# The last token tiles of a mixer: T1's work first, sums beside copies, and a fixed place for the last transposes

## The chip, the cores and the metric

One core of a Trainium2 chip runs the whole program. The metric is the device time of one execution in microseconds (us), lower is better. The engines are PE (TensorE), DVE (VectorE), ACT (ScalarE), POOL (GpSimd) and SP (SyncE, which only issues DMAs here). Each takes its own instructions in the order in which the program lists them.

## The reference

One layer of a decoder trunk on x, 1024 tokens by 1024 channels, in float32: a pooling mixer, then a gated feed-forward network (FFN) with hidden width 2816.

```
h = rms_norm(x, norm_mix_g)
d = per group of 256 channels: causal window mean of h (windows 2, 4, 8, 16) - h
x = x + scale * (einsum(d, pool_w) + pool_b)                 # the mixer
u = causal_depthwise_conv(rms_norm(x, norm_ffn_g) @ w_in)    # 3 taps, 1024 -> 2 x 2816
val, gate = split(u)
x = x + (silu(gate) * val) @ w_out                           # 2816 -> 1024
```

## The kernel before

**The mixer** runs over 8 tiles of 128 tokens (`j` = 0 to 7). For each tile `mixer_window` makes window means on PE (bank `psd`), `mixer_out` the group product (bank `psy`) and DVE adds it to x (L265), which gives the tile `x` that the FFN starts from; it is also stored to DRAM. `rstd_of` takes its mean square (ACT, `junk_b`) and a few operations on one column (`st_b`, L159 to L163), and `ffn_norm` scales the tile (L276, L277) into `n2_j`. `ffn_operand` turns `n2_j` on PE (eight transposes into two banks, `pst_j`, L292) and brings it into `n2f`, where channels lie on partitions.

**The FFN's products** are done by a seven-product scheme of 2 x 2 blocks, with sums of input blocks in place of the eighth product. Of the tokens' side the operands are B11, B21, B22 and the sums T1 to T4 (T1 = B11 - B12, in `n2f`); tiles 0 to 3 are one half of the tokens, 4 to 7 the other, so T1 is whole only when tile 7 has been turned. Of the weights' side they are A11, A12, A22 and the sums S1 to S4 of each block `n` of 128 hidden columns (`win`). Each product is in float32 accuracy by two halves: `split` and `split_n` make a high half on ACT (L76, L311) and a low half, the difference, on DVE (L77, L312), and `product` runs 12 matmuls of 128x512 (three for each of four slices). `STEPS` names a product's operands and its bank:

```
"P1": ("A11", "B11", "X"), "P6": ("S2", "T2", "Y"), "P5": ("S1", "T1", "Z"), "P2": ("A12", "B21", "X"),
"P7": ("S3", "T3", "Y"), "P3": ("S4", "B22", "Z"), "P4": ("A22", "T4", "Y"),
```

P6, P7 and P4 add up in one bank Y, P5 and P3 in one bank Z, P1 and P2 in X. Between two of them DVE or ACT reads what is there: after P1 ACT copies `q1` (L395); after P5 DVE makes `r` (L406); after P6 `q2` (L401, `q` in the profile); after P7 and P4 the halves of `hb` (L409, L414). PE may not go on adding to the bank before that read. `gated` then does the convolution and the gate: for `val` and for `gate` an ACT pass (L419) and two DVE passes (`conv`, L420 and L421), Silu on ACT, a DVE product, and the store.

**The order.** The program is not written engine by engine: a scheduling layer puts each engine's instructions in order, by their dependences and the order of the code; `tc.issue_after(m)` asks that what is in its block be issued after instruction `m`. `events` lists the products: P1 and P2 of blocks 0 and 1 first, which run while the mixer still works on its last tiles, then P5 and P3 of both, P6, P7 and P4 of each, and from block 2 on all seven block by block. `prep_event(k + LOOK)` prepares the operand of a later product at each step.

The third part of the kernel, the product with `w_out` (L723), is scheduled by its own list and is not touched.

Of the kernel before, what the change touches and what calls it, by code (L numbers as in the profile page):

```python
# [18 lines left out]
NS = S // P  # L19
# [29 lines left out]
def trunk_kernel(ctx: ExitStack, tc: tile.TileContext, x, consts, par, rows, pool_w, w_in, w_out, out):  # L49
# [223 lines left out]
    def ffn_norm(j):  # L273
        x1, r = n2s[j]
        n2 = n2s[j] = pp.tile([P, D], F32, tag="n2", name=f"n2_{j}", bufs=2)
        nc.vector.tensor_tensor(r[1], r[0], r[1], ALU.mult)  # L276
        nc.vector.scalar_tensor_tensor(n2, x1, r[1], gains[0], op0=ALU.mult, op1=ALU.mult)  # L277

# [8 lines left out]

    def ffn_operand(j):
        n2 = n2s.pop(j)
        ps = bank2(f"pst{j}")  # L290
        for c in range(NK):
            nc.tensor.transpose(ps[:, c * P : (c + 1) * P], n2[:, c * P : (c + 1) * P], ident)  # L292
# [9 lines left out]
        b11, b12, b21, b22 = n2f[:, lo, cols0], ps3[:, lo, :], n2f[:, hi, cols0], n2f[:, hi, cols]  # L302
        nc.scalar.activation(b22, ps3[:, hi, :], AF.Copy)
        sub(b11, b11, b12)
        split_n(nops["T1"], b11, cols0)
        sub(n2f[:, lo, cols], b22, b12)
        sub(b21, b22, b21)

    def split_n(t, src, cols=slice(None), ks=slice(None)):
        h = t[:, 0, ks, cols]  # L310
        nc.scalar.activation(h, src, AF.Copy)  # L311
        nc.vector.tensor_tensor(t[:, 1, ks, cols], src, h.bitcast(F32), ALU.subtract)  # L312

# [8 lines left out]
    def sub(out, a, b):  # L322
        nc.vector.tensor_tensor(out, a, b, ALU.subtract)  # L323

    def add(out, a, b):
        nc.vector.tensor_tensor(out, a, b, ALU.add)  # L326

# [20 lines left out]
    def prep_in(n, op):  # L348
        a11, a12, a21, a22 = (raws[n][:, i, k * NH : (k + 1) * NH] for i in range(2) for k in range(2))
        if op in ("S1", "S2") and (n, "S3") not in sums:  # L350
            s3 = sums[n, "S3"] = tmp(f"S3_{n}")
            add(s3, a11, a21)
            add(a21, a21, a22)
        if op in ("S2", "S4") and (n, "S2") not in sums:
            sums[n, "S2"] = a11
            add(a11, a21, a11)
        if op == "S4" and (n, "S4") not in sums:
            add(a12, a12, a11)
        if op == "S3":
            src = sums[n, "S3"]  # L360
        else:
            src = {"A11": a11, "A12": a12, "S1": a21, "A22": a22, "S2": a11, "S4": a12}[op]
        aops[n, op] = split(src, f"{op}s_{n}")
        if op == "A22" and n + 2 < NF:
            load_in(n + 2)

    def product(bank, a, b, opens):
        m = 0
        for k in range(4):
            ks = slice(k * P, (k + 1) * P)  # L370
            for i, l in ((0, 0), (0, 1), (1, 0)):
                nc.tensor.matmul(bank, a[:, i, ks], b[:, l, k, :], start=opens and m == 0, stop=m == 11, skip_group_check=not opens)  # L372
                m += 1

# [8 lines left out]

    def step(n, p):
        a, b, z = STEPS[p]
# [4 lines left out]
        bank = banks[n, z]  # L390
        product(bank, aops.pop((n, a)), nops[b], opens)
        tt = nc.vector.tensor_tensor
# [50 lines left out]

    def event(k):
        if k >= 4:
            prep_event(k + LOOK)
        n, p = events[k]
        step(n, p)
        if p == "P4":
            gated(n)  # L450
# [38 lines left out]
    for j in range(2, NS + 4):  # L489
# [4 lines left out]
        if 1 <= j - 2 < NS:  # L494
            mixer_out(j - 2)
        if 0 <= j - 2 < NS:
            with tc.issue_after(marks["dh1+"]):
                ffn_norm(j - 2)
        if 0 <= j - 4 < NS:
            ffn_operand(j - 4)  # L500
        if j in (4, 6):
# [5 lines left out]
        if j in (7, 8):  # L507
            sums_in(j - 7, 1)
        if j in (8, 10, 11):
            event((8, 10, 11).index(j))  # L510
        with tc.issue_after(marks["edges"]):
# [16 lines left out]
    event(4)  # L528
    for ks in halves:
        split_n(nops["B22"], b22[:, ks], ks=ks)  # L530
    event(5)
# [276 lines left out]
```

## Time and profile before

| | us |
|---|---|
| timed runs, median | 703.62 |
| timed runs, lowest and highest | 703.33, 790.45 |
| profiled execution, own time | 702.61 |
| its span, first to last instruction | 700.9 |

In the profile PE is busy for 99% of the span, DVE for 86%, ACT for 49%. A matmul's record is longer than the time that it adds to PE's stream, since matmuls overlap, so busy time there says little; starts are the better measure. Names in a row are the program's, without numbers: `q` is any `q1` or `q2`, `n` any `n2_j`, `T` any of T1 to T4, `B` any of B11, B21, B22. A row's brackets give the idle time of its engine ahead of it, and the instruction that ended that.

The stretch that the change touches lies from about 58 us (the transposes of tile 4) to about 130 us (block 2's products); of 700.9 us the rest is the mixer's first tiles, the other blocks, and the product with `w_out`.

### The profile page before, as it was taken

Reading aid. Unit: us, or ns where it says so; the run is one execution under the profiler, and the core shown is the slowest. Engines: PE = TensorE matmul, PEld = TensorE weight load, DVE = VectorE, ACT = ScalarE, POOL = GpSimd, SP = SyncE. Lnnn points to the kernel's source line nnn. Section 1 sums busy time; section 2 is a strip of 40 time slices with the busy share of each in tenths; the row PEclk is TensorE's granted clock in tenths of the full one; section 3 lists DMA queues with packets and bytes.
Section 4 is the critical chain, followed back from the end, with each engine's and each line's share of the span. In section 5 each row is a group of like instructions: output and inputs, shape, how many; then the busy total and the mean of one; then the engine's idle time right before and its main releaser. Section 6 shows DMA issues by size and latency. Waiting matters only on the chain.

```text
span 700.9 us, 8493 instructions
## 1 busy us (share of the span) xinstructions
PE 693.9 (99%) x3154; PEld 573.7 (82%) x3154; DVE 600.5 (86%) x885; ACT 343.2 (49%) x515; POOL 12.5 (2%) x30
## 2 busy tenths in 40 slices
PE   8999999999999999999999999999999999999998
PEld 5898778888888888888888888888888888888886
DVE  5688999999888888888988888876887988999985
ACT  4786545454444444444545454454554444444431
POOL 3110000000000000000000000000000000000000
PEclk9999999999999999999999999999999999999999
DMA  9854112232222112222222212229989700122131
GB/s 307 302 141 121 57 65 91 89 122 91 67 84 74 60 78 90 91 90 91 91 90 91 86 65 91 91 84 338 335 305 335 277 22 1 61 90 87 64 106 60
DMA packets 32555, 85.47 MB, mean 122 GB/s; under 512 B 3689, under 2 KB 5377, under 8 KB 29698
## 3 DMA queue, kind: packets, MB, share of 16 engines
q1 hardware_dynamic: 31296, 82.82, 32.8%
q0 software_dynamic: 1184, 2.11, 1.8%
q8 instruction: 24, 0.39, 0.2%
q14 instruction: 17, 0.14, 0.1%
q10 hardware_dynamic: 34, 0.01, 0.0%
HBM read 62.89 MB, written 19.92 MB: 118 GB/s over the span
## 4 chain that ended last, share of the span: by engine, by line
PE 96%; DVE 2%; DMA 1%; ACT 1%; issue 0%; ACTq 0%; DVEq 0%
PE oP L723 30%; PE Y L372 26%; PE Z L372 17%; PE X L372 16%; PE psy L259 3%; PE psd L180 2%; DMA bias_hl<-rows_raw 1%; PE pst L292 1%; PE psy L262 1%; DVE n2f L323 0%; DMA x<-in_x_dram 0%; DVE T L312 0%; PE ps_edges L180 0%; PE ps_gain L227 0%; DVE n L277 0%; DVE S4s L77 0%
## 5 line engine op out<-in xcount | busy, mean ns | idle before, releaser
L723 PE MATMUL oP<-oBP,oAP 128*128 128x512 f32 (+1 forms) x924 | 208.8, 388 | 0.0
L723 PEld LDWEIGHTS oP<-oBP,oAP 128*128 128x128 f32 x924 | 172.9, 188 | 36.0 <-DVE oBP L77 0.3
L372 PE MATMUL Z<-T,S1s 128*128 128x512 f32 x264 | 64.0, 390 | 1.4 <-ACT T L311 1.2
L372 PE MATMUL X<-B,A11s 128*128 128x512 f32 x264 | 64.3, 390 | 0.0
L372 PE MATMUL Y<-T,S2s 128*128 128x512 f32 x264 | 64.0, 390 | 0.0
L372 PE MATMUL X<-B,A12s 128*128 128x512 f32 x264 | 63.5, 389 | 0.0
L372 PE MATMUL Y<-T,S3s 128*128 128x512 f32 x264 | 63.4, 389 | 0.0
L372 PE MATMUL Y<-T,A22s 128*128 128x512 f32 x264 | 63.4, 389 | 0.0
L372 PE MATMUL Z<-B,S4s 128*128 128x512 f32 x264 | 63.2, 389 | 0.0
L372 PEld LDWEIGHTS Z<-T,S1s 128*128 128x128 f32 x264 | 49.3, 188 | 12.6 <-ACT T L311 1.6
L372 PEld LDWEIGHTS Y<-T,S2s 128*128 128x128 f32 x264 | 49.4, 188 | 10.8 <-ACT S2s L76 0.4
L372 PEld LDWEIGHTS Y<-T,S3s 128*128 128x128 f32 x264 | 49.5, 188 | 10.3
L372 PEld LDWEIGHTS Z<-B,S4s 128*128 128x128 f32 x264 | 49.5, 188 | 10.3
L372 PEld LDWEIGHTS Y<-T,A22s 128*128 128x128 f32 x264 | 49.5, 188 | 10.3
L372 PEld LDWEIGHTS X<-B,A12s 128*128 128x128 f32 x264 | 49.5, 188 | 10.2
L372 PEld LDWEIGHTS X<-B,A11s 128*128 128x128 f32 x264 | 49.4, 188 | 10.2
L76 ACT ACTIVATE oBP<-blk 128x512 fp32r<-128x512 f32 x53 | 33.5, 633 | 49.1 <-PE oP L723 32.2
L77 DVE TENSOR_TENSOR oBP<-blk,oBP 128x512 fp32r<-128x512 f32 x53 | 36.6, 691 | 13.3 <-ACT oBP L76 13.3
L430 ACT ACTIVATE gate<-gate 128x1024 f32<-128x1024 f32 x22 | 23.3, 1061 | 44.5 <-DVE gate L421 44.5
L76 ACT ACTIVATE oAP<-blk 128x512 fp32r<-128x512 f32 x55 | 34.1, 621 | 19.2 <-DVE blk L323 15.9
L326 DVE TENSOR_TENSOR win<-win 128x512 f32<-128x512 f32 x60 | 41.3, 688 | 1.1
L77 DVE TENSOR_TENSOR oAP<-blk,oAP 128x512 fp32r<-128x512 f32 x55 | 37.7, 685 | 2.6 <-ACT oAP L76 2.6
(128 smaller groups left out, 941.4 us busy)
## 6 DMA issues: line engine op xcount, KB each, us to landing
win<-in_w_in_dram SPq DMA_DIRECT2D x22, 1024.0 KB, 4.8
g_dram<-val SPq DMA_DIRECT2D x22, 512.0 KB, 2.7
blk<-g_dram SPq DMA_DIRECT2D x33, 256.0 KB, 5.4
blk<-in_w_out_dram SPq DMA_DIRECT2D x31, 256.0 KB, 5.6
A12s<-g_dram SPq DMA_DIRECT2D x22, 256.0 KB, 5.3
B21s<-in_w_out_dram SPq DMA_DIRECT2D x22, 256.0 KB, 2.6
x<-in_x_dram SPq DMA_DIRECT2D x8, 512.0 KB, 7.0
x_dram<-x SPq DMA_DIRECT2D x8, 512.0 KB, 2.6
```

Of the source, the lines that this page charges most:

```text
L76: nc.scalar.activation(t[:, 0, :], src, AF.Copy)
L77: m = nc.vector.tensor_tensor(t[:, 1, :], src, t[:, 0, :].bitcast(F32), ALU.subtract)
L180: m = nc.tensor.matmul(ps[:, c * P : (c + 1) * P], src[:, c * P : (c + 1) * P], weights[:, c // 2, :], start=True, stop=True)
L259: nc.tensor.matmul(o, dh[:, c, :], wps[:, c, :], start=c % 4 == 0, stop=False, skip_group_check=True)
L262: m = nc.tensor.matmul(ps[:, cols], ones, bias_hl[:, cols], start=False, stop=True, skip_group_check=True)
L292: nc.tensor.transpose(ps[:, c * P : (c + 1) * P], n2[:, c * P : (c + 1) * P], ident)
L326: nc.vector.tensor_tensor(out, a, b, ALU.add)
L372: nc.tensor.matmul(bank, a[:, i, ks], b[:, l, k, :], start=opens and m == 0, stop=m == 11, skip_group_check=not opens)
L430: nc.scalar.activation(gate, gate, AF.Silu)
L723: nc.tensor.matmul(bank, a[:, u, i * P : (i + 1) * P], b[:, v, c], start=opens and first, stop=g == NP2 - 1 and m == 2, skip_group_check=n ...
```

## The change

Eight things change, all in the code around the mixer's last tiles.

- `ffn_operand` is cut in two: `ffn_turn` (the transposes, and for tiles 4 to 7 the copy of the upper four slices on ACT) and `ffn_operand` (the rest). `ffn_last` holds the last sum, on B21.
- In `ffn_operand` the two sums that read the transposes' bank come first, then T1's split; for tiles 6 and 7 `ffn_last` is left for later.
- The norm of tile 7 is issued after T1's split of tile 5; the transposes of tile 6 and 7 get a place by hand: tile 7's stand inside block 0's P2, behind three of its four slices (`between`).
- The operands of P5 (S1 of blocks 0 and 1) are prepared right after tile 6's norm.
- `gated(0)` is issued after block 2's S2 sum.
- B22 is split right after T1's last split, ahead of the sums on B21 and of the other preparations; before, it stood behind `event(4)`.
- The pool `ps_yz` gives out one bank, named "lower", that nothing uses, before Z's first banks.
- `event(3)` is issued after the last transposes.

```diff
+    def ffn_turn(j):
         n2 = n2s.pop(j)
         ps = bank2(f"pst{j}")
         for c in range(NK):
-            nc.tensor.transpose(ps[:, c * P : (c + 1) * P], n2[:, c * P : (c + 1) * P], ident)
-        cols = slice(j * P, (j + 1) * P)
-        ps3 = ps.rearrange("p (c s) -> p c s", c=NK)
+            m = nc.tensor.transpose(ps[:, c * P : (c + 1) * P], n2[:, c * P : (c + 1) * P], ident)
+        marks["turned"] = m.ins
+        turned[j] = ps.rearrange("p (c s) -> p c s", c=NK)
+        if j >= NS // 2:
+            nc.scalar.activation(n2f[:, 4:, j * P : (j + 1) * P], turned[j][:, 4:, :], AF.Copy)
+        return m.ins
+
+    def ffn_operand(j, last=True):
+        ps3, cols = turned[j], slice(j * P, (j + 1) * P)
...
-        nc.scalar.activation(b22, ps3[:, hi, :], AF.Copy)
         sub(b11, b11, b12)
-        split_n(nops["T1"], b11, cols0)
-        sub(n2f[:, lo, cols], b22, b12)
-        sub(b21, b22, b21)
+        m = sub(n2f[:, lo, cols], b22, b12)
+        if last:
+            m = ffn_last(j)
+        with tc.issue_after(m):
+            marks[f"T1_{j}"] = split_n(nops["T1"], b11, cols0)
...
+    def ffn_last(j):
+        b21, b22 = (n2f[:, 4:, t * P : (t + 1) * P] for t in (j - NS // 2, j))
+        return sub(b21, b22, b21)
...
-    def product(bank, a, b, opens):
-        m = 0
+    def product(bank, a, b, opens, between):
+        m, order = 0, nullcontext()
         for k in range(4):
             ks = slice(k * P, (k + 1) * P)
-            for i, l in ((0, 0), (0, 1), (1, 0)):
-                nc.tensor.matmul(bank, a[:, i, ks], b[:, l, k, :], start=opens and m == 0, stop=m == 11, skip_group_check=not opens)
-                m += 1
+            with order:
+                for i, l in ((0, 0), (0, 1), (1, 0)):
+                    last = nc.tensor.matmul(bank, a[:, i, ks], b[:, l, k, :], start=opens and m == 0, stop=m == 11, skip_group_check=not opens)
+                    m += 1
+            if between and k == 2:
+                with tc.issue_after(last.ins):
+                    order = tc.issue_after(between())
...
-        if p == "P4":
+        if p == "P4" and n == 0:
+            with tc.issue_after(marks["S2_2"]):
+                gated(n)
+        elif p == "P4":
             gated(n)
...
+        if j == 9:
+            ffn_turn(5)
+            with tc.issue_after(marks[7]):
+                ffn_operand(5)
+            with tc.issue_after(marks["T1_5"]):
+                ffn_norm(7)
+        elif j == 10:
+            ffn_turn(6)
+        else:
...
+        if j == 8:
+            with tc.issue_after(marks["n2_6"]):
+                prep_event(4)
+                prep_event(5)
+            event(0)
+        if j == 10:
+            event(1)
+        if j == 11:
+            event(2, between=lambda: ffn_turn(7))
+            with tc.issue_after(marks["n2_7"]):
+                ffn_operand(6, last=False)
+                with tc.issue_after(marks["T1_6"]):
+                    ffn_operand(7, last=False)
...
+    ps_yz.tile([P, NH], F32, tag="Y", name="lower")
...
-    for k in range(4, 4 + LOOK):
-        with tc.issue_after(marks[NS - 1]):
-            prep_event(k)
...
-    event(3)
+    with tc.issue_after(marks["T1_7"]), tc.issue_after(marks["split_hi"]):
+        prep_event(6)
+        for ks in halves:
+            m = split_n(nops["B22"], b22[:, ks], ks=ks)
+    with tc.issue_after(m):
+        for j in (6, 7):
+            ffn_last(j)
+        for k in range(7, 4 + LOOK):
+            prep_event(k)
+    with tc.issue_after(marks["turned"]):
+        event(3)
     event(4)
-    for ks in halves:
-        split_n(nops["B22"], b22[:, ks], ks=ks)
     event(5)
```

How the engines' orders move is shown at three places; in these rows names carry their numbers (a number behind a name's last `_` is the buffer's).

PE before, from tile 6's transposes to the first products into Z (`X0` is block 0's bank X, and so on):

```order
L292 MATMUL pst6_713<-cst_81,n2_6_637 128x128 x8
L372 MATMUL X1_728<-B11_162,A11s_1_546 128x512 x12
L372 MATMUL X0_660<-B21_164,A12s_0_600 128x512 x12
L372 MATMUL X1_728<-B21_164,A12s_1_655 128x512 x3
L292 MATMUL pst7_743<-cst_81,n2_7_695 128x128 x8
L372 MATMUL X1_728<-B21_164,A12s_1_655 128x512 x9
L372 MATMUL Z0_819<-T1_163,S1s_0_787 128x512
L372 MATMUL Z1_843<-T1_163,S1s_1_790 128x512
L372 MATMUL Z0_819<-T1_163,S1s_0_787 128x512 x11
```

PE after the change, the same place:

```order
L294 MATMUL pst6_719<-cst_81,n2_6_637 128x128 x8
L388 MATMUL X1_729<-B11_162,A11s_1_546 128x512 x12
L388 MATMUL X0_666<-B21_164,A12s_0_600 128x512 x9
L294 MATMUL pst7_753<-cst_81,n2_7_716 128x128 x8
L388 MATMUL X0_666<-B21_164,A12s_0_600 128x512 x3
L388 MATMUL X1_729<-B21_164,A12s_1_655 128x512 x12
L388 MATMUL Z0_824<-T1_163,S1s_0_660 128x512 x12
L388 MATMUL Z1_844<-T1_163,S1s_1_663 128x512 x12
```

Tile 7's transposes move ahead by six matmuls, and the two products into Z no longer mix.

DVE before, behind the sum of tile 7 (`x7`), which stands right ahead of these rows:

```order
L77 TENSOR_TENSOR S1s_0_787<-win0_415,S1s_0_787 128x512
L323 TENSOR_TENSOR n2f_161<-n2f_161,pst5_698 128x4x128 x2
L323 TENSOR_TENSOR n2f_161<-n2f_161 128x4x128
L160 TENSOR_SCALAR st_b7_689<-st_b7_689 128x1
L312 TENSOR_TENSOR T1_163<-n2f_161,T1_163 128x4x128
L162 SCALAR_TENSOR_TENSOR st_b7_689<-st_b7_689 128x1
L323 TENSOR_TENSOR n2f_161<-n2f_161,pst6_713 128x4x128
L163 RECIPROCAL st_b7_689<-st_b7_689 128x1
L323 TENSOR_TENSOR n2f_161<-n2f_161,pst6_713 128x4x128
L276 TENSOR_TENSOR st_b7_689<-st_b7_689 128x1
L323 TENSOR_TENSOR n2f_161<-n2f_161 128x4x128
L277 SCALAR_TENSOR_TENSOR n2_7_695<-x7_152,st_b7_689,gain_b_266 128x1024
```

DVE after the change, from the place where S1's two low halves now stand:

```order
L77 TENSOR_TENSOR S1s_0_660<-win0_415,S1s_0_660 128x512
L77 TENSOR_TENSOR S1s_1_663<-win1_540,S1s_1_663 128x512
L265 TENSOR_TENSOR x7_152<-psy7_681,x7_152 128x1024
L337 TENSOR_TENSOR n2f_161<-n2f_161,pst5_701 128x4x128 x2
L337 TENSOR_TENSOR n2f_161<-n2f_161 128x4x128
L160 TENSOR_SCALAR st_b7_695<-st_b7_695 128x1
L326 TENSOR_TENSOR T1_163<-n2f_161,T1_163 128x4x128
L162 SCALAR_TENSOR_TENSOR st_b7_695<-st_b7_695 128x1
L163 RECIPROCAL st_b7_695<-st_b7_695 128x1
L276 TENSOR_TENSOR st_b7_695<-st_b7_695 128x1
L277 SCALAR_TENSOR_TENSOR n2_7_716<-x7_152,st_b7_695,gain_b_266 128x1024
```

Both S1 halves move ahead of `x7`, and the sums of tile 6 move from between the one-column steps to behind `n2_7`.

DVE before, around the read of Y2 after block 2's P6 (`q2_2`), in the midst of blocks 1 and 2 (`hb1` and `gate33` are block 1's, `r_2` block 2's):

```order
L414 TENSOR_TENSOR hb1_1011<-q1_1_741,Y1_980 128x512
L77 TENSOR_TENSOR S4s_2_1041<-win2_841,S4s_2_1041 128x512
L77 TENSOR_TENSOR A22s_2_1059<-win2_841,A22s_2_1059 128x512
L401 TENSOR_TENSOR q2_2_1077<-Y2_1064,q1_2_1057 128x512
L420 SCALAR_TENSOR_TENSOR gate33_1033<-hb1_1011,par_sb_121,gate33_1033 128x1023
L77 TENSOR_TENSOR A11s_3_1079<-win3_897,A11s_3_1079 128x512
L421 SCALAR_TENSOR_TENSOR gate33_1033<-hb1_1011,par_sb_121,gate33_1033 128x1022
L406 TENSOR_TENSOR r_2_1095<-q1_2_1057,Z2_1082 128x512
```

DVE after the change, the same place:

```order
L433 TENSOR_TENSOR hb1_1012<-q1_1_742,Y1_981 128x512
L440 SCALAR_TENSOR_TENSOR val11_1030<-ha1_819,par_sb_121,val11_1030 128x1022
L340 TENSOR_TENSOR win2_842<-win2_842 128x512
L439 SCALAR_TENSOR_TENSOR gate33_1034<-hb1_1012,par_sb_121,gate33_1034 128x1023
L77 TENSOR_TENSOR S4s_2_1042<-win2_842,S4s_2_1042 128x512
L440 SCALAR_TENSOR_TENSOR gate33_1034<-hb1_1012,par_sb_121,gate33_1034 128x1022
L77 TENSOR_TENSOR A22s_2_1060<-win2_842,A22s_2_1060 128x512
L420 TENSOR_TENSOR q2_2_1078<-Y2_1065,q1_2_1058 128x512
```

The two passes on `gate33` move from behind `q2_2` to ahead of it.

More of the change, by code (lines that the diff above doesn't have):

```diff
@@ L286, in trunk_kernel @@
         nops[b] = nop_tile(nop_a, b)
-    def ffn_operand(j):
+    turned = {}
+    def ffn_turn(j):
         n2 = n2s.pop(j)
@@ L322, in sub @@
     def sub(out, a, b):
-        nc.vector.tensor_tensor(out, a, b, ALU.subtract)
+        return nc.vector.tensor_tensor(out, a, b, ALU.subtract).ins
     def add(out, a, b):
-        nc.vector.tensor_tensor(out, a, b, ALU.add)
+        return nc.vector.tensor_tensor(out, a, b, ALU.add).ins
     def tmp(name):
@@ L355, in prep_in @@
             sums[n, "S2"] = a11
-            add(a11, a21, a11)
+            marks[f"S2_{n}"] = add(a11, a21, a11)
         if op == "S4" and (n, "S4") not in sums:
@@ L382, in small, with step @@
         return work.tile([P, NH], F32, tag=tag, name=name, bufs=bufs)
-    def step(n, p):
+    def step(n, p, between=None):
         a, b, z = STEPS[p]
@@ L390, in step @@
         bank = banks[n, z]
-        product(bank, aops.pop((n, a)), nops[b], opens)
+        product(bank, aops.pop((n, a)), nops[b], opens, between)
         tt = nc.vector.tensor_tensor
@@ L442, in prep_event, with event @@
             prep_in(n, STEPS[p][0])
-    def event(k):
+    def event(k, between=None):
         if k >= 4:
@@ L447, in event @@
         n, p = events[k]
-        step(n, p)
-        if p == "P4":
+        step(n, p, between)
+        if p == "P4" and n == 0:
+            with tc.issue_after(marks["S2_2"]):
+                gated(n)
+        elif p == "P4":
             gated(n)
@@ L495, in trunk_kernel @@
             mixer_out(j - 2)
[L496 to L500, printed above, removed]
+        if j == 9:
[7 more added lines that the diff above has]
+        else:
+            if 0 <= j - 2 < NS:
+                with tc.issue_after(marks["dh1+"]):
+                    ffn_norm(j - 2)
+            if 0 <= j - 4 < NS - 1:
+                ffn_turn(j - 4)
+                ffn_operand(j - 4)
         if j in (4, 6):
```

10 lines of the change are left out of this document (4 added, 6 removed).

## The prediction

> **What bounds the kernel now.** I read the page first, then the chain of work that ended last.
>
> ```profile
> PE 693.9 (99%) x3154; PEld 573.7 (82%) x3154; DVE 600.5 (86%) x885; ACT 343.2 (49%) x515; POOL 12.5 (2%) x30
> PE 96%; DVE 2%; DMA 1%; ACT 1%; issue 0%; ACTq 0%; DVEq 0%
> ```
>
> TensorE (PE) is the path for 96% of the span, so whatever moves the end must lengthen or shorten a stretch in which PE waits or restarts. The chain leaves PE for some 12 us near 67 to 79.5 us: work of VectorE (DVE) and ScalarE (ACT) that ends in T1's last low half.
>
> ```profile
> 72.77 1.28 DVE n L277
> 78.80 0.67 DVE T L312
> 79.51 10.71 PE Z L372 x46
> ...
> 118.30 2.73 PE Y L372 x12
> ```
>
> PE is not idle all that time. Its timeline there (start, length, idle time and what ended it in brackets), and the one row of PE on which the sum below ends:
>
> ```profile
> 75.01 2.33 PE L372 MATMUL X<-B,A12s 128*128 128x512 f32 x9
> 78.55 0.73 PE L372 MATMUL Z<-T,S1s 128*128 128x512 f32 x2 [1.21 <-ACT T L311]
> 79.51 5.27 PE L372 MATMUL Z<-T,S1s 128*128 128x512 f32 x22 [0.23 <-DVE T L312]
> ...
> 118.14 2.89 PE L372 MATMUL Y<-T,S3s 128*128 128x512 f32 x12
> ```
>
> One matmul adds 2.73 / 12 = 0.227 us to the chain. From 75.01 to 79.51 PE started nine matmuls and two more, and 11 x 0.227 = 2.50 of those 4.50 us: **2.0 us is all that there is to win here**, 1.44 us of it shown as idle. Besides these two, the list of what PE waited for has three entries, all at the kernel's start:
>
> ```profile
> PE idle_ps L130 <- DVE eps_t L108: 1.3, 1, 1.3
> PE psy L259 <- ACT dh L244: 0.6, 1, 0.6
> ...
> PE psy L262 <- DMA bias_hl<-rows_raw: 0.2, 1, 0.2
> ```
>
> Before asking whether the change wins the 2.0 us, I ask which engine is behind it: from x7's sum at 66.37 us on, DVE waits for nothing but 0.1 us at a `q`.
>
> ```profile
> DVE x L265 <- PE psy L262: 1.4, 1, 1.4
> L401 DVE TENSOR_TENSOR q<-Y,q 128x512 f32<-128x512 f32 x3 | 2.0, 683 | 0.1
> ```
>
> So DVE, not PE, is short of time from 66 to 118 us. PE follows it wherever a bank must be read before PE may add to it again. The place that matters is `q2_2`: DVE must read Y2 after P6 before PE may start P7 into Y2.
>
> ```profile
> 117.24 0.68 DVE L401 TENSOR_TENSOR q<-Y,q 128x512 f32<-128x512 f32 x1
> 117.84 1.27 DVE L420 SCALAR_TENSOR_TENSOR gate<-hb,par_sb,gate 128x1023 f32<-128x1023 f32 x1
> 119.03 0.68 DVE L77 TENSOR_TENSOR A11s<-win,A11s 128x512 fp32r<-128x512 f32 x1
> ```
>
> `q2_2` ends at 117.92, and P7 starts at 118.14: now 0.2 us are to spare. The first of two `gate` operations stands right behind it, the second behind A11s.
>
> **The change, part by part.** I take DVE's queue from x7's sum to `q2_2`, since DVE takes its instructions in order and had no slack there.
>
> *What stands in it.* By the order, 67 instructions lie between the two before and 67 after. Two go, S1s_0 and S1s_1: the change puts both ahead of x7's sum, into the wait in brackets.
>
> ```profile
> 66.37 1.22 DVE L265 TENSOR_TENSOR x<-psy,x 128x1024 f32<-128x1024 f32 x1 [1.42 <-PE psy L262]
> 67.51 0.68 DVE L77 TENSOR_TENSOR S1s<-win,S1s 128x512 fp32r<-128x512 f32 x1
> 68.11 1.28 DVE L323 TENSOR_TENSOR n2f<-n2f,pst 128x512 f32<-128x512 f32 x2
> ```
>
> Each takes 68.11 - 67.51 = 0.60 us of the queue, 1.20 together, which fits into 1.42: free, and x7's sum still starts at 66.37. Were that cover gone, they would cost their 1.20. Two come in, the `gate` pair of block 1, which moves ahead of `q2_2`: 119.03 - 117.84 = 1.19 us each, 2.38. **Net +1.18 us.**
>
> *Small operations.* In T1's old order sums of tile 6 stand between tile 7's one-column steps; now these follow one another. The same steps of tile 6 show what that costs, and tile 7's own rows what it costs now:
>
> ```profile
> 63.02 0.21 DVE L162 SCALAR_TENSOR_TENSOR st_b<-st_b 128x1 f32<-128x1 f32 x1
> ...
> 63.66 1.28 DVE L277 SCALAR_TENSOR_TENSOR n<-x,st_b,gain_b 128x1024 f32<-128x1024 f32 x1
> ...
> 70.71 0.21 DVE L162 SCALAR_TENSOR_TENSOR st_b<-st_b 128x1 f32<-128x1 f32 x1
> 70.84 0.68 DVE L323 TENSOR_TENSOR n2f<-n2f,pst 128x512 f32<-128x512 f32 x1
> 71.44 0.16 DVE L163 RECIPROCAL st_b<-st_b 128x1 f32<-128x1 f32 x1
> ```
>
> Bare, 63.66 - 63.02 = 0.64; between sums 0.13 + 0.07 + 0.06 = 0.26 (70.84 - 70.71, and the like behind the next two, which take 0.60 each). **+0.38 us.** In return n2_7 runs at 71.1 instead of 72.77.
>
> *Waits for ACT that DVE did not have.* "Sums while ScalarE copies" puts a DVE operation right behind the ACT operation it needs. I take 0.03 us from end to start, from these two rows (93.59 + 1.22 = 94.81, against 94.84):
>
> ```profile
> 93.59 1.22 DVE L326 TENSOR_TENSOR n2f<-n2f 128x1024 f32<-128x1024 f32 x1
> 94.84 1.06 ACT L311 ACTIVATE T<-n2f 128x1024 fp32r<-128x1024 f32 x1 [3.94 <-DVE n2f L326]
> 67.24 0.60 ACT L303 ACTIVATE n2f<-pst 128x512 f32<-128x512 f32 x1 [3.67 <-PE pst L292]
> 69.44 0.63 ACT L311 ACTIVATE T<-n2f 128x512 fp32r<-128x512 f32 x1
> 75.29 0.60 ACT L303 ACTIVATE n2f<-pst 128x512 f32<-128x512 f32 x1
> 75.97 2.00 ACT L311 ACTIVATE B<-n2f 128x1024 fp32r<-128x1024 f32 x2
> ```
>
> Tile 5's first sum needs the copy: 67.24 + 0.60 + 0.03 = 67.87 against DVE free at 67.51, 0.36. T1's low halves of tiles 6 and 7 need the high half, which needs the first sum: 0.68 + 0.03 + 0.63 + 0.03 = 1.37, of which the two sums cover 1.20: 0.17 each. Tile 7's sum needs its copy, which starts 75.29 - 74.19 = 1.10 us behind the first transpose. That one now follows nine matmuls of X0's P2:
>
> ```profile
> 70.67 3.56 PE L372 MATMUL X<-B,A12s 128*128 128x512 f32 x15
> 74.19 1.06 PE L292 MATMUL pst<-cst,n 128*128 128x128 f32 x8
> ```
>
> So 70.67 + 9 x 0.227 + 1.10 + 0.63 = 74.44, while DVE is through with n2_7 (71.1 + 1.19), two sums, the 0.17 and a split at 74.26: 0.2. B22's first half needs an ACT pass of 1.05 behind T1's and S4s_0's, while DVE has only their two low halves of 0.60 to do: 77.29 against 77.03 by my estimate, 0.26. Together **+1.16 us**; none is seen in the trace of before, so I bound them by nothing and by twice that.
>
> *A wait for PE.* Block 1's second `hb` reads Y1 after P4 and now stands ahead of the `gate` pair. PE starts Y0's P4 behind block 0's first `hb`:
>
> ```profile
> 99.93 0.68 DVE L409 TENSOR_TENSOR hb<-r,Y 128x512 f32<-128x512 f32 x1
> ```
>
> Up to there DVE has -1.20 + 0.38 + 1.16 - 0.1 (the wait at `q`, which goes) = +0.24, so PE starts at 99.93 + 0.24 + 0.71 = 100.9. By the new order P4 into Y1 ends 58 matmuls on, at 114.2 (57 x 0.227, and 2.89 - 11 x 0.227 + 0.03 = 0.42 for the last one to be seen). Without a wait `q2_2` would start at 119.86, and the second `hb` stands seven operations (four of 0.60, three of 1.19) or 5.97 us ahead of that, at 113.9: **+0.3 us**.
>
> *The sum.* 1.18 + 0.38 + 1.16 + 0.3 - 0.1 = 2.9: `q2_2` starts at 120.16 instead of 117.24, and PE's P7 into Y2 at 120.16 + 0.71 = 120.87 instead of 118.14: **2.7 us later**. The same matmuls stand before it in both orders, so the early gain doesn't reach the end: with pst7 ahead of X0's last three products, T1 is whole near 76.5 and PE goes from P2 to P5 at 77.1 without a wait (-2.0); then it waits 0.5 to 0.9 us for `r_0` (the order puts it behind B22's low halves and three splits, so near 82.6), about 1.0 for block 0's `hb` at Y0's P4, and 3 us around X3's P1 and Y2's P7. Behind it DVE has the `gate` pair done, and I see no later wait, so the 2.7 stays to the end.
>
> *Edits that I cost at nothing.* The unused bank "lower" only changes numbers of banks; Z's first matmul waits for T1 either way. B22 split sooner is needed at 83 and done at 77.3 + 2 x 1.13 = 79.6. The loads on SP's queue: block 2's still follows A22s_0's low half, some tenths later than now, with over ten us until its first use; block 4's follows A22s_2's low half and goes out near 120.3 instead of 117.34, lands 4.8 later, and is first read near 125.1, eight operations behind `q2_2`: the two just meet. Were it late, DVE would wait some tenths, with 5 us in hand before PE needs block 3's operands. POOL's queue is unchanged.
>
> ```profile
> 117.34 0.33 SPq L320 DMA_DIRECT2D win<-in_w_in_dram  x1
> win<-in_w_in_dram SPq DMA_DIRECT2D x22, 1024.0 KB, 4.8
> ```
>
> [...] PE would wait twice with two matmuls between, 3 us in all. How PE runs cold shows at the kernel's start, where the same matmul takes 3.59 / 8 = 0.45 us at first and 1.03 / 4 = 0.26 later:
>
> ```profile
> 1.26 3.59 PE L130 MATMUL idle_ps<-idle 128*128 128x512 bf16 x8 [1.26 <-DVE eps_t L108]
> 9.44 1.03 PE L130 MATMUL idle_ps<-idle 128*128 128x512 bf16 x4
> ```
>
> Behind the 1.21 us wait of Z's P5 the matmuls did not slow down: from 79.51 on 22 of them took 5.27 us, 0.24 each. [...]
>
> **Rivals.** *The gain survives* (not slower): P5 without its wait ends 2.0 us earlier and nothing takes it back: 702.6 - 2.0 = 700.6 by the profiled execution. It needs `q2_2` to start 1.8 us before 117.24, and DVE's queue has 1.18 more in it: only the 1.42 us at x7's sum could give it, and the S1s take 1.20 of that. *A draw*: ACT runs far enough ahead that none of the 1.16, 0.38 and 0.3 shows; then P7 is late by 1.18 - 0.1 - 0.2 = 0.9 at most, less what a faster DVE makes up: 702.6 to 703.5. *The clock falls* in the wait near 119: a cold stretch like that of the start, eight matmuls in 3.59 us instead of 8 x 0.227, loses 1.8 us more: 702.6 + 2.7 + 1.8 = 707.1. It decides once PE stays idle longer than the 1.2 us that did no harm. *Slower by more than 2%*: B22 and its siblings lie where x2 to x6 lay, and ACT now waits for the stores of these to land before B22, with T2 and T3 queued behind; x6's sum is done before x7's at 66.37, and B22 starts near 76, so 14 us more would need a store of over 23 us:
>
> ```profile
> x_dram<-x SPq DMA_DIRECT2D x8, 512.0 KB, 2.6
> ```
>
> **How the numbers follow.** The profiled execution took 702.61 us; 2.7 more is 705.3. The runs shown have 703.62 as their median, so 706.3 by that; I take 705.8, between the two. Ends: without the small terms (0.38, 1.16, 0.3) +0.9, with them doubled +4.6, so 703.5 to 708.2; the draw is let in at the lower end, the gain is not. Chances: forecast 0.74, gain 0.09, draw 0.09, clock 0.06, over 2% slower 0.02. About 2% (14 us) is what a measurement of this kernel can tell from no change, so nearly all of it is "within".
>
> **What would show it.** Right: PE without idle at Z's P5; DVE without the 1.42 us at x7's sum; waits of PE at Z0's P3, Y0's P4 and above all Y2's P7 on `q`, started near 120.8. Wrong: Y2's P7 before 118, or `q2_2` at 118 with PE not waiting; or new waits behind 125 us.

## The result, and the profile after

| | before | after |
|---|---|---|
| timed runs, median (lowest to highest), us | 703.48 (702.68 to 790.45) | 707.97 (706.41 to 709.74) |
| ratio after / before, 95% interval | | 1.0066 (1.0047 to 1.0085) |
| profiled execution, own time, us | 702.61 | 706.46 |
| its span, us | 700.9 | 704.7 |

The change makes the kernel some 0.7% slower: within the 2% that the prediction called no change, but measurably so. A second series of six runs gave 708.10 against 703.06, ratio 1.0065 (1.0049 to 1.0080). The run of 790.45 is a disturbed one and is left out of the ratio. The changed kernel's times come in two groups: where the granted clock of the whole run is 0.999 or 1.000, four runs of the twelve, they are 706.4 to 706.7; where it is 0.995 or 0.997, the other eight, 707.4 to 709.8. The profile shown first is of the former kind.

The page's lines on busy time and on the chain that ended last:

```profile
PE 693.1 (98%) x3154; PEld 573.3 (81%) x3154; DVE 601.5 (85%) x885; ACT 343.4 (49%) x515; POOL 12.5 (2%) x30
PE 94%; DVE 3%; DMA 1%; ACT 1%; issue 0%; ACTq 0%
```

PE's share of the chain falls by two points of a hundred. PE's timeline says where (start, length, idle time and what ended it):

```profile
73.34 1.03 PE L294 MATMUL pst<-cst,n 128*128 128x128 f32 x8
74.13 3.67 PE L388 MATMUL X<-B,A12s 128*128 128x512 f32 x15
77.64 5.60 PE L388 MATMUL Z<-T,S1s 128*128 128x512 f32 x24
83.97 5.72 PE L388 MATMUL Z<-B,S4s 128*128 128x512 f32 x24 [0.73 <-ACT S3s L76]
101.63 3.00 PE L388 MATMUL Y<-T,A22s 128*128 128x512 f32 x12 [0.94 <-ACT val L438]
119.40 0.73 PE L388 MATMUL X<-B,A11s 128*128 128x512 f32 x2 [1.17 <-ACT A11s L76]
121.83 3.03 PE L388 MATMUL Y<-T,S3s 128*128 128x512 f32 x12 [1.70 <-DVE q L420]
124.69 2.88 PE L388 MATMUL Z<-B,S4s 128*128 128x512 f32 x12
```

The last transposes stand inside P2 as written, Z's P5 follows at 77.64 with no idle time (before 1.21 and 0.23), and then PE waits four times, 4.54 us in all, the longest time for `q2_2`. In two of the brackets the last to end is an ACT operation that the product does not read: P3 at 83.97 needs Z0 free, that is DVE's `r_0` (83.19 to 83.87), and P4 at 101.63 needs Y0 free, block 0's `hb` (100.80 to 101.48). That these two are what PE waits for follows from the program; the profile names S3s and `val`. Behind 124.69 the list of PE's waits has no further entry.

Executions differ by some 2 us ahead of block 0's first product. Before and after differ there by 0.61, all of it in the first 17 us, in PE's waits for the first DMAs (0.17 us before, 1.45 + 0.45 after) and in how long the matmuls around them take (eight of `idle_ps` 3.59 and 3.27, four of `ps_scale` 2.62 and 1.96). So two profiles are best compared from a point behind that. I take the start of block 0's first product, and from there to the start of the kernel's last group of matmuls. Before, after and (further down) after again:

```profile
59.41 3.00 PE L372 MATMUL X<-B,A11s 128*128 128x512 f32 x12
696.28 1.24 PE L723 MATMUL rest<-oBP,oAP 128*128 128x256 f32 x9
60.02 3.02 PE L388 MATMUL X<-B,A11s 128*128 128x512 f32 x12
700.12 1.24 PE L773 MATMUL rest<-oBP,oAP 128*128 128x256 f32 x9
59.33 3.01 PE L388 MATMUL X<-B,A11s 128*128 128x512 f32 x12
701.02 1.24 PE L773 MATMUL rest<-oBP,oAP 128*128 128x256 f32 x9
```

That distance is 636.87 before and 640.10 after: **+3.23 us**, of 3.85 by the executions' own times; the other 0.6 is the start. In the second profile of the changed kernel it is 641.69, 1.59 more. Every "distance" below is this one.

DVE's timeline after, at the places that the prediction's sum is made of:

```profile
65.47 1.29 DVE L77 TENSOR_TENSOR S1s<-win,S1s 128x512 fp32r<-128x512 f32 x2
66.99 1.23 DVE L265 TENSOR_TENSOR x<-psy,x 128x1024 f32<-128x1024 f32 x1 [0.23 <-PE psy L262]
68.49 1.29 DVE L337 TENSOR_TENSOR n2f<-n2f,pst 128x512 f32<-128x512 f32 x2 [0.28 <-ACT n2f L298]
...
113.37 1.23 DVE L450 TENSOR_TENSOR val<-val,gate 128x1024 f32<-128x1024 f32 x1
115.10 0.69 DVE L433 TENSOR_TENSOR hb<-q,Y 128x512 f32<-128x512 f32 x1 [0.50 <-PE Y L388]
...
117.50 1.28 DVE L439 SCALAR_TENSOR_TENSOR gate<-hb,par_sb,gate 128x1023 f32<-128x1023 f32 x1
...
119.29 1.28 DVE L440 SCALAR_TENSOR_TENSOR gate<-hb,par_sb,gate 128x1022 f32<-128x1022 f32 x1
...
121.09 0.69 DVE L420 TENSOR_TENSOR q<-Y,q 128x512 f32<-128x512 f32 x1
```

From x7's sum to `q2_2` it is 121.09 - 66.99 = 54.10 us, before 117.24 - 66.37 = 50.87: +3.23. That the distance grows by the same number to the hundredth is partly chance. Of the 3.23, 0.16 was time to spare between `q2_2` and P7 (118.14 - 117.24 = 0.90 before, 121.83 - 121.09 = 0.74 after), and P7 behind its wait takes 0.14 more (3.03 against 2.89 before). But the size agrees: PE got DVE's lateness and little else.

### The profile page after: what moved, and what is told of

Read it like the earlier page. It is cut to its first block, busy times and chain, and to the rows that moved or that the text cites. A ratio compares the mean times of both kernels' runs of the same rounds, so it can differ in the third digit from the quotient of the medians.

```text
span 704.7 us, 8504 instructions
## 1 busy us (share of the span) xinstructions
PE 693.1 (98%) x3154; PEld 573.3 (81%) x3154; DVE 601.5 (85%) x885; ACT 343.4 (49%) x515; POOL 12.5 (2%) x30
## 4 chain that ended last, share of the span: by engine, by line
PE 94%; DVE 3%; DMA 1%; ACT 1%; issue 0%; ACTq 0%
PE oP L773 30%; PE Y L388 24%; PE Z L388 17%; PE X L388 16%; PE psy L259 3%; PE psd L180 2%; DMA bias_hl<-rows_raw 1%; PE pst L294 1%; DVE T L326 1%; PE psy L262 1%; DMA x<-in_x_dram 0%; DVE n2f L340 0%; PE ps_edges L180 0%; PE ps_gain L227 0%; DVE q L420 0%
```

## The experiments

The theory: DVE's order up to `q2_2` sets the end, and the gain at Z's P5 is given back there. Its first rival: PE's waits add up, so that each one removed is worth its length. A second question came with the result: what makes the upper group of runs. A table of all kernels first (distance as above; low clock: runs with a granted clock of 0.997 or less).

| kernel | median us, beside before | ratio, 95% | distance, against before | low clock |
|---|---|---|---|---|
| changed kernel | 707.97, 703.48 | 1.0047 to 1.0085 | +3.23 | 3 of 6 |
| the same again | 708.10, 703.06 | 1.0049 to 1.0080 | +4.82 | 5 of 6 |
| 1 gate pair held back | 704.21, 703.25 | 1.0001 to 1.0020 | +0.77 | 0 of 12 |
| 2 the same, nothing in its place | 705.04, 703.53 | 1.0013 to 1.0032 | +1.70 | 1 of 12 |
| 3 before, gate pair moved alone | 706.72, 703.06 | 1.0031 to 1.0060 | +2.74 | 1 of 6 |
| 4 S1s pair back | 708.71, 703.06 | 1.0055 to 1.0090 | +4.96 | 5 of 6 |
| 5 val and gate behind `q2_2` | 704.45, 703.25 | 1.0009 to 1.0027 | +1.44 | 0 of 11 |
| 6 early waits removed only | 708.09, 703.25 | 1.0045 to 1.0075 | +5.41 | 5 of 5 |
| 7 as 6, PE kept at work | 707.01, 703.53 | 1.0029 to 1.0057 | +3.48 | 0 of 6 |
| 8 changed kernel, PE kept at work | 706.25, 703.06 | 1.0028 to 1.0053 | +3.23 | 0 of 5 |
| 9 all moved | 701.36, 703.25 | 0.9960 to 0.9981 | -2.04 | 0 of 9 |
| 9 again | 701.75, 703.59 | 0.9961 to 0.9981 | -1.96 | 0 of 10 |
| 10 before, with the order of 9 from B22 on | 702.29, 703.59 | 0.9969 to 0.9993 | -1.21 | 0 of 12 |

**1 and 2: the gate pair, undone.**

```diff
+        elif p == "P4" and n == 1:
+            gated_val(n)
...
+        if (n, p) == (2, "P6"):
+            with tc.issue_after(marks["q2_2"]):
+                gated(1)
```

> The changed kernel, with only block 1's two gate operations held behind q2_2 again (A22s_2's low half stays ahead of it). Theory (DVE's queue up to q2_2 sets the end; the pair is 2.38 us of it): q2_2 starts near 118.7 instead of 121.1, PE's wait for it ahead of Y2's P7 goes, and of the waits behind 117 us only some 0.5 for A11s_3 is left, so about 2.4 us less than the changed kernel: 704.0 by its profiled 706.46. Rival (what is late is not that queue but the earlier waits of PE, 0.7 for r_0 and 0.9 for hb): they stay, the time stays near 706.5. If the second group of the changed kernel's runs (709.3 to 709.7 beside 706.4 to 706.7) is TensorE's clock falling in the wait of 1.2 + 1.7 us near 119, it should vanish here.

The distance fell by 2.46 against the changed kernel, as expected, and no run shows the low clock; but it did not come by the expected way. DVE and PE there:

```profile
119.61 0.68 DVE L423 TENSOR_TENSOR q<-Y,q 128x512 f32<-128x512 f32 x1
118.07 0.73 PE L390 MATMUL Z<-B,S4s 128*128 128x512 f32 x2
119.11 0.50 PE L390 MATMUL X<-B,A11s 128*128 128x512 f32 x1 [0.31 <-ACT A11s L76]
119.45 1.55 PE L390 MATMUL Z<-B,S4s 128*128 128x512 f32 x6
120.83 2.88 PE L390 MATMUL Y<-T,S3s 128*128 128x512 f32 x12
```

`q2_2` is not near 118.7. The scheduling layer put `r_2` and one of block 3's sums into the freed place, and with `r_2` early PE had eight matmuls of Z2's P3 to do ahead of Y2's P7. So I took that away too (r_2 and block 3's sums held behind `q2_2`, PE's order as in the changed kernel):

```diff
+                    held = (n, p) == (2, "P3") or ((n, p) == (3, "P1") and m > 1)
+                    with tc.issue_after(marks["p7"]) if held else nullcontext():
...
+        with tc.issue_after(marks["q2_2"]) if k in (16, 17) else nullcontext():
+            event(k)
```

> As the first experiment (block 1's gate pair behind q2_2), but with nothing else moved into its place: r_2 and block 3's sums are held behind q2_2, and PE keeps P7 of Y2 ahead of the rest of X3's P1 and of Z2's P3, as in the changed kernel. In the first one DVE filled the place with r_2 and a sum (0.60 each), so q2_2 came only 1.2 us sooner, and PE did eight matmuls of Z2's P3 ahead of P7. Theory: the pair leaves 2.38 us; of these DVE waits some 0.6 to 0.8 for ScalarE at S4s_2, which the pair covered; PE's second wait near 119 falls from 1.7 to 0.2 to 0.4 us and the end lies 1.6 to 1.8 us before the changed kernel without its clock's fall (706.5): 704.8. Rival (the first experiment's gain came from PE's order alone): 706.5.

```profile
117.55 0.69 DVE L77 TENSOR_TENSOR S4s<-win,S4s 128x512 fp32r<-128x512 f32 x1 [0.76 <-ACT S4s L76]
118.76 0.68 DVE L427 TENSOR_TENSOR q<-Y,q 128x512 f32<-128x512 f32 x1
119.50 3.02 PE L392 MATMUL Y<-T,S3s 128*128 128x512 f32 x12 [0.16 <-DVE q L427]
```

1.53 less than the changed kernel (1.6 to 1.8 expected): 2.38 less the 0.76 for which DVE now waits for ScalarE. The rival, that the first gain came from PE's order alone, falls. The other 0.9 of the 2.46 came with `r_2`, block 3's sum and PE's eight matmuls in the freed place; these were not taken apart.

**3: the gate pair, done alone in the kernel before.**

```diff
-            tt(hid[n, "q2"], bank, hid[n, "q1"], ALU.subtract)
+            with tc.issue_after(marks[f"gate{NF + order[1]}"]) if n == 2 else nullcontext():
+                tt(hid[n, "q2"], bank, hid[n, "q1"], ALU.subtract)
```

> The kernel before, with one thing changed: block 1's two gate operations stand ahead of q2_2, as in the changed kernel (what follows q2_2 is held there). Theory: DVE reads Y2 2.4 to 2.7 us later (2 x 1.19 and up to 0.3 for ScalarE's pass of the gate), 0.2 of it was spare, PE waits near 2.5 us ahead of P7 and the end is 2.2 to 2.7 us later than the kernel before: 705.5 to 706.0 where that takes 703.3. A wait of 2.5 us in one piece should not bring the clock down, since in the kernel with only the early waits removed it fell some 3.5 us after PE's last matmul: granted clock 1.0 behind it. Rival (a later block makes up for it, or PE has other work to do meanwhile): 703.3.

```profile
121.62 3.01 PE L374 MATMUL Y<-T,S3s 128*128 128x512 f32 x12 [2.39 <-DVE q L406]
```

One wait, of 2.39 us, and a distance longer by 2.74, at the upper edge of 2.2 to 2.7. This one move, without any of the rest, costs most of what the whole change costs. The expectation on the clock did not hold throughout: one of the six runs shows 0.997, and so does one of experiment 2's twelve, where PE's longest wait behind the start is 1.2 us. Neither of these two runs was profiled, so where their clock fell is not shown.

**4: the S1s pair, undone.**

```diff
-            with tc.issue_after(marks["n2_6"]):
-                prep_event(4)
-                prep_event(5)
...
+            with tc.issue_after(marks[7]):
+                prep_event(4)
+                prep_event(5)
```

> The changed kernel with the two S1s low halves back behind x7's sum, where the kernel before has them (one of them, by then). By the prediction's term the two are worth 1.20 us at q2_2, less what the operations behind them no longer wait for ScalarE (up to 0.4 at tile 5's copy, and DVE's wait for x7's sum comes back): 0.7 to 1.2 us more than the changed kernel, its lower group near 707.2 to 707.7. Rival (the 1.42 us wait at x7's sum was never free time, since another wait takes its place): no difference, 706.5. With PE's wait longer by that much, the upper group should hold more of the runs.

```profile
67.16 1.23 DVE L265 TENSOR_TENSOR x<-psy,x 128x1024 f32<-128x1024 f32 x1 [1.42 <-PE psy L262]
68.30 1.28 DVE L77 TENSOR_TENSOR S1s<-win,S1s 128x512 fp32r<-128x512 f32 x2
69.50 1.28 DVE L337 TENSOR_TENSOR n2f<-n2f,pst 128x512 f32<-128x512 f32 x2
122.41 4.34 PE L390 MATMUL Y<-T,S3s 128*128 128x512 f32 x12 [1.70 <-DVE q L422]
118.40:121.80 3.40, 1.15 (x4) 0.30 (x2) 3.40 (x5) 2.56 (x5) 0.00 (x0) 1.00 0.00 0
```

The 1.42 us wait is back, and the pair stands behind it. P7 starts 122.41 - 60.20 = 62.21 after block 0's first product (60.20 in this profile), 61.81 in the changed kernel: the pair's place is worth **0.40**, not 0.7 to 1.2. Behind it the sum of tile 5 no longer waits (0.36 in the changed kernel), nor does that of tile 7 (0.25); the last 0.2 of the pair's 1.20 is mostly (0.12) shorter gaps between tile 7's one-column steps, where one more operation, the sum on B21, now stands. The one run at full clock, 707.37, lies in the expected 707.2 to 707.7, but single times differ by more than that with their start. The rest of the distance, 1.33, is the clock: twelve matmuls in 4.34 us, behind a stretch of 3.40 us (the last row) with PE busy for 1.15 of it, and with a granted clock of 0.51 in the 3.45 us after that.

**5: `q2_2` ahead of all of block 1's val and gate operations.** As experiment 1, but with `gated(1)` as a whole behind `q2_2`:

```diff
-        elif p == "P4":
+        elif p == "P4" and n > 1:
             gated(n)
+        if (n, p) == (2, "P6"):
+            with tc.issue_after(marks["q2_2"]):
+                gated(1)
```

> The changed kernel, with block 1's val and gate operations all held behind q2_2, so that DVE reads Y2 some 9 us sooner. Theory (DVE is short, not late at one place): q2_2 near 112.5, no wait of PE for it, but A11s_3's low half now stands behind the four operations of block 1 and PE waits about 1.1 us for it in X3's P1; end about 1.9 us before the changed kernel: 704.5. Rival (only the place of q2_2 matters): no wait behind 110 us at all, 703.3 or less.

```profile
118.14 2.88 PE L388 MATMUL Y<-T,S3s 128*128 128x512 f32 x12
122.49 0.97 PE L388 MATMUL X<-B,A11s 128*128 128x512 f32 x3 [1.02 <-DVE A11s L77]
```

1.79 less than the changed kernel, as the theory had it: `q2_2` starts at 112.86, PE has no wait for it, and the next one up is A11s_3, whose low half DVE reaches behind the four operations. The rival, no wait at all behind 110 us, falls.

**6 and 9: the early waits alone, and everything.** Kernel 9 writes DVE's order from B22 on by what PE needs next; 6 is the same but for one line, which leaves val and gate of blocks 1 and 2 where the changed kernel has them. The core of it:

```diff
+    with tc.issue_after(marks["r_0"]):
+        prep_event(7)
+        prep_event(8)
...
+            with tc.issue_after(marks["hb_0"]):
+                for e in (12, 15, 13):
+                    prep_event(e)
...
+        if n - 1 in LATE and p == "P5":
+            with tc.issue_after(marks[f"A11s_{n + 1}"]):
+                gate_of(n - 1)
+        if n - 1 in LATE and p == "P2":
+            with tc.issue_after(marks[f"S2s_{n + 1}"]):
+                val_of(n - 1)
...
+    LATE = (1, 2)
```

In kernel 6 the last line is `LATE = ()`.

> As the kernel with all moved, but block 1's and block 2's val and gate operations left where the changed kernel has them. Theory: the waits for r_0 and for hb (0.7 and 0.9 us with their restarts 1.9) go, and all of it comes back in one wait of about 4.5 us at X3's P1 for A11s_3's low half near 119 to 123.8; end as the changed kernel, 706.5. Rival (PE's waits add up): 704.6. On the clock: if TensorE's granted clock falls after some 3 to 4 us of idling, all of its runs, not half of them, should lie some 2.9 us higher, near 709.4; if the second group has another cause, two groups as before.

PE at the one wait that is left of those behind the start, and stretches of time around it (PE busy with its matmuls, PEld, DVE, ACT, POOL, then the granted clock, DMA share and GB/s):

```profile
123.58 0.79 PE L390 MATMUL X<-B,A11s 128*128 128x512 f32 x1 [4.31 <-DVE A11s L77]
124.18 5.44 PE L390 MATMUL Z<-B,S4s 128*128 128x512 f32 x12
119.00:122.40 3.40, 0.27 (x2) 0.00 (x0) 3.40 (x5) 1.65 (x2) 0.00 (x0) 1.00 0.00 0
122.40:125.80 3.40, 2.22 (x5) 1.62 (x6) 3.40 (x6) 0.00 (x0) 0.00 (x0) 0.53 0.97 251
125.80:129.25 3.45, 3.45 (x10) 2.68 (x9) 2.28 (x5) 2.19 (x4) 0.00 (x0) 0.50 0.55 209
```

The waits for `r_0` and `hb` are gone and came back in one of 4.31 us at A11s_3. All five runs show the low clock; without it (2.77, from experiment 7) the distance would be 0.59 below the changed kernel's, where the theory said 0 and the rival 1.9. So of the 1.9 won early two thirds were given back, not all. Then the clock took it and more. It fell some 0.2 us into the second stretch shown (0.53 is the mean of 0.2 us at 1.00 and the rest at 0.50), 3.3 us after PE's last matmul had ended at 119.27.

> The changed kernel, with DVE's order from B22 on written so that each operation stands where PE needs it: r_0 right behind B22's two sums, T2 before S3s_0 and A22s_0, S3s_1 and A22s_1 and block 2's sums behind block 0's hb, the two ha sums with their val pair, block 1's gate pair behind A11s_3, its val pair behind S2s_3, the same for block 2. No operation is added or left out. Theory (the early gain of 2.0 us is real and is given back only because DVE's order puts work that nobody waits for ahead of what PE waits for): no wait of PE over 0.25 us behind 78 us, q2_2 near 113.7, end 4.9 us before the changed kernel: 701.6 by its profile, 2 us below the kernel before on the same chip. Rival (DVE has too much to do at all, in any order): waits come up again behind 120 us and the time is 704 or more.

What PE waited for in kernel 9, the whole list, and two rows of it:

```profile
PE idle_ps L130 <- DVE eps_t L108: 1.3, 1, 1.3
PE ps_scale L200 <- DMA rows_raw<-in_rows_dram: 0.8, 1, 0.8
PE psy L259 <- ACT dh L244: 0.6, 1, 0.6
PE psy L262 <- issue: 0.2, 1, 0.2
77.08 5.60 PE L390 MATMUL Z<-T,S1s 128*128 128x512 f32 x24
113.42 0.68 DVE L422 TENSOR_TENSOR q<-Y,q 128x512 f32<-128x512 f32 x1
```

All four are at the kernel's start. With the same operations in another order the list has no wait of PE behind 16 us, `q2_2` is read at 113.42, and the distance is 2.04 us (1.96 in the repeat) below that of the kernel before: the 2.0 that the prediction found as all there is to win. The rival, that DVE has too much to do in any order, falls.

**10: how much of that is the change's own work on the last tiles.** The kernel before, with the lines of kernel 9 from B22 on, and this ahead of them. (Two of the change's smaller edits come along with these lines: B22's split ahead of `event(4)`, and `gated(0)` behind block 2's S2.)

```diff
-    for k in range(4, 4 + LOOK):
+    for k in range(4, 7):
         with tc.issue_after(marks[NS - 1]):
             prep_event(k)
```

> The kernel before with its own way through the mixer's last tiles (old T1 order, last transposes behind fifteen matmuls, S1s pair split as it was), but with the order of the kernel with all moved from B22 on; S4s_1, S2s_0 and later splits so come behind r_0 instead of between T1's sums. It tells how much of the 2 us of that kernel is the change's own work on the last tiles. Theory: the order from B22 on can win only what lies ahead of Z's P5, and there S4s_1 and S2s_0 (2 x 0.60 on DVE) no longer stand ahead of T1's last low half: PE's waits of 1.21 and 0.23 us fall to some 0.3 each, 1.2 to 1.5 us less than the kernel before, 701.8 where that takes 703.2. Rival A (the change's work on the last tiles brings all of it): 703.2, waits as before. Rival B (the order alone brings all of it): 701.2.

> The kernel with all moved once more, beside the kernel before with the same late order on the same chip: 701.3 again, 0.5 to 0.9 us below that one if the change's work on the last tiles is worth what is left of PE's waits at Z's P5.

```profile
77.83 6.15 PE L374 MATMUL Z<-T,S1s 128*128 128x512 f32 x24 [0.25 <-ACT T L311]
```

1.21 of the 2.0 come without the change: with S4s_1 and S2s_0 no longer ahead of T1's last low half, P5 waits 0.25 instead of 1.21 and 0.23. The change's own part is the other 0.8 (0.54 by the medians of the two, on one chip). Kernel 10 loses it at the wait that is left and inside P5, whose 24 matmuls take 6.15 us here and 5.60 in kernel 9.

**7 and 8: the clock.** First the changed kernel again.

> The changed kernel itself once more, for the size of its second group of runs. Theory (TensorE's granted clock falls in some executions, in the wait of two parts near 118 to 122 us): about half of the times near 706.5, half near 709.5, and where the profiled one is of the upper half, its granted clock is 0.5 for some 7 us from near 122 us on and the matmuls there take 0.43 us. Rival (the upper half has another cause, such as a later start): the granted clock stays at 1.0 there.

```profile
121.15 4.61 PE L388 MATMUL Y<-T,S3s 128*128 128x512 f32 x12 [1.70 <-DVE q L420]
118.29:121.70 3.41, 1.28 (x4) 0.78 (x5) 3.41 (x5) 1.92 (x3) 0.00 (x0) 1.00 0.17 19
121.70:125.12 3.42, 3.42 (x9) 2.63 (x8) 2.40 (x4) 0.00 (x0) 0.00 (x0) 0.50 0.82 313
125.12:128.53 3.41, 3.41 (x16) 2.82 (x15) 2.74 (x5) 0.21 (x1) 0.00 (x0) 1.00 0.32 129
```

Five of the six runs lie in the upper group, and this execution is one of them, with a clock of 0.997. The granted clock is 0.50 from 121.70 to 125.12, half of the 7 us expected, and P7 takes 4.61 us instead of 3.03: the 1.58 is the whole difference of the two distances (1.59). Then PE was given ten matmuls of no use in the wait:

```diff
+        if (n, p) == (2, "P2"):
+            some = nops["B11"].rearrange("p a k s -> p (a k s)").bitcast(BF16)
+            spare = ps_yz.tile([P, NH], F32, tag="Z", name="spare")
+            with tc.issue_after(marks["mm"].ins):
+                for _ in range(10):
+                    m = nc.tensor.matmul(spare, some[:, :P], some[:, :NH], start=True, stop=True)
```

> The changed kernel with ten more matmuls (128x512, bf16, into an unused bank) put between X2's P2 and Y2's P7, where PE waits 1.2 + 1.7 us: 10 x 0.26 = 2.6 us of work in a gap of 3.3, so that PE is hardly idle there. Theory (the clock): one group of times near 706.5, none near 709.5, clock 0.999 in every run. Rival: both groups as before. If the added matmuls hold up P7, the time is some tenths over 706.5, in one group.

No run of five shows the low clock, and the distance is +3.23 to the hundredth, that of the changed kernel's undisturbed profile. The same in kernel 6, with fifteen, behind the second matmul of X3's P1:

```diff
+                    if (n, p) == (3, "P1") and m == 2:
...
+                            for _ in range(15):
+                                marks["warm"] = nc.tensor.matmul(spare, some[:, :P], some[:, :NH], start=True, stop=True).ins
```

> The kernel with only the early waits removed, with fifteen matmuls more (128x512, bf16, into an unused bank) in its wait of 4.3 us at X3's P1: 15 x 0.227 = 3.4 us. Theory (the clock falls because PE idles there, and only that): granted clock 1.0 behind 122 us, the twelve matmuls that took 5.44 us take 2.9, all runs some 2.8 us lower: 705.3. Rival (the clock falls for another reason at that time of the program): 708.1 as before.

```profile
121.00 3.41 PE L398 MATMUL spare<-B 128*128 128x512 bf16 x15
125.49 0.98 PE L391 MATMUL X<-B,A11s 128*128 128x512 f32 x3 [1.07 <-DVE A11s L77]
126.30 2.91 PE L391 MATMUL Z<-B,S4s 128*128 128x512 f32 x12
142.45 3.01 PE L391 MATMUL Y<-T,S3s 128*128 128x512 f32 x12 [0.55 <-DVE q L429]
```

The twelve matmuls take 2.91 instead of 5.44, and block 3's first product P6 starts 2.77 sooner, counted from block 0's first product (133.35 - 61.54 against 134.23 - 59.65). The end gains only 1.93, not 2.8: a wait of 0.55 for block 3's `q` appears, which experiment 6's profile, with the slow matmuls ahead of it, does not have. By the medians it is 1.1 (708.09 and 707.01, on two chips). The rival, another cause at that time of the program, falls for both kernels.

## Why the prediction was right, and where it was not

- **No idle time at Z's P5, and the gain lost by Y2's P7**: right. P5 at 77.64 is 17.62 after block 0's first product; before, the 22 matmuls behind the second wait started 20.10 after it, two others being done, so P5 is 20.10 - 0.45 - 17.62 = 2.0 sooner, as said. The waits came where named: `r_0` 0.73 (0.5 to 0.9), `hb` 0.94 (about 1.0), around X3's P1 and Y2's P7 1.17 + 1.70 (3). P7 starts 61.81 after block 0's first product instead of 118.14 - 59.41 = 58.73: 3.08 later, where 2.7 was said.
- **The sum**: 2.9 at `q2_2`, measured 3.23. Instructions: said 1.18, measured 1.19 (the `gate` pair 1.19 and 1.20, the S1s pair 0.60 each). Waits for ACT: said 1.16, measured 0.36, 0.19, 0.25, 0.19 and 0.26 = 1.25; one of 0.17 ahead of a T low half was not foreseen. Small operations: said 0.38, measured 0.23; the sum left out that DVE already lost 0.13 there, between the first one-column step and T1's low half. The wait at `hb`: said 0.3, measured 0.58 (115.10 against 113.37 + 1.15), the largest miss. The wait at `q`: said -0.1, measured -0.16. With the 0.17 these make 3.26, 0.03 off by rounding.
- **"S1s... free", -1.20**: right as bookkeeping and wrong as a price. Undone it is worth 0.40, since 0.6 of the waits for ACT exist only because the pair no longer stands in front of them, and 0.2 went in the steps behind. Likewise the `gate` pair's 2.38 are 1.53 when taken out and 2.74 when put in alone. Terms on one in-order queue are not independent.
- **"DVE, not PE, is short of time from 66 to 118 us"**: half right. DVE has next to no idle time there, and in the given order it is late. But kernel 9 shows that it is not short of time: every read that PE needs fits 2 us sooner, with the same operations. The rival "the gain survives" was judged by the queue's length (it "has 1.18 more in it") instead of by what in it PE needs before 118 us.
- **The clock** is the step that failed. It got 0.06 and was left out of the forecast: that 3 us with two matmuls in them would not bring the clock down was my estimate, and no run had shown it. The clock fell in 8 of 12 runs, by the clock of the whole run; one of them was profiled. Its price, 1.8, was near the measured 1.58, where the clock stayed at 0.50 for 3.42 us; where it stayed there for some 6.8, as in experiment 6, it is 2.77. The price was taken from the kernel's start, where the record of the granted clock reads 1.00, so that the slow matmuls there (0.45 us each) don't by themselves show a low clock. By the median the clock is most of the miss: 705.8 forecast, 707.97 measured. The execution with a full clock, 706.46, belongs beside the 705.3 that was worked out from the profiled one: 1.2 above, 0.6 of it the start and 0.5 the sum.
- **That the median lies within 703.5 to 708.2** is in part luck. The upper end came from doubling the small terms, which turned out near their size; the clock, which had no place in the range, used up the room, all but 0.23 us.
- **Block 4's load** met its first read within 0.34 us of wait on DVE, and PE did not see it, as said. The other edits costed at nothing showed no wait of PE; none was tried alone.

## What to carry to other kernels

When an engine's queue is full, ask of each instruction in front of a late one who needs it and when, before calling the engine the bound: here a gain of 2 us was lost, and won again, by order alone. Price a moved instruction by taking it out and by putting it in, since waits behind it open and close. A wait on TensorE of some 3 us should be counted with the slow matmuls that may follow it (twelve in 4.61 us instead of 3.03 behind waits of 1.17 and 1.70 here), and in two kernels here cheap matmuls into an unused bank kept that away.

## What the runs showed of the hardware

- TensorE's granted clock fell from 1.00 to 0.50 at 121.70 us in the second profile of the changed kernel, near 121.9 in experiment 4 and near 122.6 in experiment 6. Ahead of the fall PE was still busy for 1.28 of 3.41 us (changed kernel), 1.15 of 3.40 (experiment 4) and 0.27 of 3.40 (experiment 6, up to 122.40). The clock stayed at 0.50 for 3.42, some 3.4 and some 6.8 us; in experiment 6 PE was busy for 2.22 of the 3.40 us from 122.40 on. PE's work in a stretch does not decide it alone: in the changed kernel's execution at full clock PE was busy for only 0.73 of the 3.41 us behind 118.23, and the clock stayed at 1.00. Why the same wait brings the clock down in some executions and not in others, no run here shows.
- Twelve matmuls of 128x512 in float32 took 2.88 us at full clock and 5.44 in experiment 6's slow stretch. Behind a wait they took some 0.15 more even at full clock: P7 3.03 behind its wait of 1.70, P3 right after it 2.88.
- Block 0's first product started between 59.24 and 61.54 us in these 14 profiles, although PE's work ahead of it is the same in all: single executions have to be compared from behind the start.
